# Five pairs of weight blocks multiplied with seven block products in place of eight

## The chip, the core and the metric

The kernel runs on one core of one Trainium2 chip. The metric is the device time of one execution in microseconds (us), the median over several runs. Before the change it is 1874.03 us (three runs, 1873.88 to 1874.24).

## What is computed

The reference is a trunk of two layers over 256 tokens of 2048 channels, in float32. Each layer normalises the input, projects it with one wide matrix, runs a convolution branch and an attention branch, and merges both. Only the end of a layer matters here:

```python
y_conv = conv_branch(...) @ w_proj_conv          # (256, 2048) @ (2048, 2048)
y_mla = mla_branch(...) @ w_proj_mla
y = jax.nn.sigmoid(g_conv) * y_conv + jax.nn.sigmoid(g_mla) * y_mla
return x + y @ w_out                             # (256, 2048) @ (2048, 2048)
```

The two products with `w_proj_conv` (called pconv below) and `w_out` (called wout) are the last two projections of a layer.

## The kernel before

**Work and tiles.** Each projection is a list of blocks of 512 output columns: pconv and wout have four each, and they come last in a layer, in the order pmla 0 to 3, pconv 0 to 3, wout 0 to 3. Behind wout 3 of layer 0 comes the block glu 0 of layer 1. A block is fed by eight pieces of weights. A piece is two K tiles of 128 rows (`KS = 2`) by 512 columns, 512 KB in float32. The 256 tokens are two halves of 128 (`t`).

**Split terms.** Float32 accuracy is had from operands in the fp32r format. Both sides are split into a high and a low part, and of the four products three are computed: high x high, low activation x high weight, high activation x low weight. A piece therefore costs two halves by two K tiles by three terms, twelve matmuls of 512 columns, all accumulated in two PSUM banks, one for each half.

**How a piece gets there.** SP's queue loads it into one of five buffers `raw` (`load`, line 185). ScalarE copies it to `hi`, which rounds it (`split_hi`, line 194, four buffers). VectorE subtracts, `lo = raw - hi` (`split_lo`, line 230, three buffers). `product` (line 362) goes through the pieces: for piece i it issues `hi` up to i+3, `lo` up to i+2 and loads up to i+7, then the matmuls, then `background` (line 266). The order of the twelve matmuls is that of `order_of_products` (line 303): the eight with the high weights first, then the four with the low ones. The last piece of a block ends the first half earlier.

**The order of everything else.** Every engine runs its instructions in the order in which the program issues them (class `InOrder`, line 121). Work beside the matmuls is a list `steps` of functions with the clock at which they are due, one tick of the clock for each piece. `background` runs what is due, in the order of the list. `at_slot(n, f)` (line 247) puts a function n ticks ahead at the end of the list; the evacuation of a block is put at the front (line 394), due one tick after the block's end, or in its last tick for pconv 3 and wout 3.

**Evacuation.** `pconv_evac` (line 1245) multiplies each half in PSUM by a gate and adds another tile (four VectorE instructions of 512 columns, called gates below). The result must be transposed for wout: `turn` (line 418) writes it to DRAM in four transfers, fetches it back 4 ticks later into a tile `turned` of the pool `wide`, has VectorE transpose it 8 ticks later, and one tick later ScalarE and VectorE split it into the high and low parts of `yT`. `turn4` (line 1159) shortens this to 2 and 4 ticks for the last block. `wout_evac` (line 1274) does the same with the layer's output in layer 0, adds the residual `xres`, and makes `hT`, the activations of layer 1, with eight short instructions on ScalarE and eight on VectorE for each block. The last block of layer 1 goes through `last_product` (line 319).

**PSUM.** Four banks are `acc` (two blocks in turn), two are `tp` and one is `s0`, both used by attention only.

Of the kernel before, what the change touches and what calls it, by code (L numbers as in the profile page):

```python
# [11 lines left out]
F32 = mybir.dt.float32  # L12
F32R = mybir.dt.float32r
# [6 lines left out]
P = 128  # L20
T = 2
# [48 lines left out]

REVOLUTION_PIECES = 6


def revolution_pieces():

# [42 lines left out]
def trunk(ctx: ExitStack, tc: tile.TileContext, xT, x, g_in, pos, win, wuq, wukv, wpc, wpm, wo, cst, rows, invf, out):  # L118
# [43 lines left out]
    pieces = []  # L162

    def plan(layer, stream):
        ap, nk = streams[stream]
        i, at = taken.get((layer, stream), (0, 0))
        n = blocks_of_layer()[stream][i]
        mine = []
        for g in range(nk // KS):
            size = P * KS * n  # L170
            pieces.append((ap[layer, at : at + size].rearrange("(p k c) -> p k c", p=P, k=KS), n))
            at += size
            mine.append(len(pieces) - 1)
        taken[layer, stream] = (i + 1, at)
        return nk, n, mine


    plans = []
    for l in range(DEPTH):
        plans.append([(k, i, plan(l, s)) for k, i, s in order_of_layer()])  # L180

    loaded, highs, pairs_of, done, blocks_begun = {}, {}, {}, {}, [0]
    LOAD_AHEAD, HI_AHEAD, LO_AHEAD = 4, 3, 2

    def load(i):
        if i >= len(pieces) or i in loaded:
            return
        ap, n = pieces[i]
        loaded[i] = t = raw_p.tile([P, KS, n], F32, tag="raw", name=f"raw{i}")
        for a in range(0, KS, 1 if i < N_SINGLE else KS):  # L190
            k = slice(a, a + 1 if i < N_SINGLE else KS)
            sp.dma_start(t[:, k, :], ap[:, k, :])

    def split_hi(i):
        if i >= len(pieces) or i in highs:
            return
        load(i)
        n = pieces[i][1]
        paired = n == PAIRED
        both = split_p.tile([P, KS, 2 * n if paired else n], F32R, tag="hi", name=f"hi{i}", bufs=4)  # L200
        highs[i] = both[:, :, :n]
        if paired:
            pairs_of[i] = both
        singly = i < N_SINGLE
        if i == 0:
            one = [slice(a, a + 1) for a in range(KS)]
            scale_x(0, "hi", vec)
            scale_x(0, "lo", vec)
            act.copy(highs[i][:, one[0]], loaded[i][:, one[0]])
            scale_x(1, "hi", vec)  # L210
            act.copy(highs[i][:, one[1]], loaded[i][:, one[1]])
            split_lo(i, one[0])
            scale_x(1, "lo", vec)
            split_lo(i, one[1])
        for a in () if i == 0 else range(0, KS, 1 if singly else KS):
            k = slice(a, a + 1 if singly else KS)

            if singly:
                act.copy(highs[i][:, k], loaded[i][:, k])
            for c in range(min(i * KS + k.start, NCT), min(i * KS + k.stop, NCT)):  # L220
                scale_x(c, "hi", act)
                scale_x(c, "lo", vec)
            if singly:
                split_lo(i, k)
            else:
                act.copy(highs[i][:, k], loaded[i][:, k])
        for a in range(1, LOAD_AHEAD + 1):
            load(i + a)

    def split_lo(i, k=slice(0, KS)):  # L230
        if i >= len(pieces) or done.get(i, (0, 0, 0))[2] >= k.stop:
            return
        n = pieces[i][1]
# [4 lines left out]
        vec.tensor_sub(lo[:, k], loaded[i][:, k], highs[i][:, k].bitcast(F32))  # L238
        done[i] = highs[i], lo, k.stop


# [21 lines left out]
    def mark(name):  # L263
        marks[name] = clock[0]

    def background(n):
        clock[0] += 1
        slot = (8 * (1.5 * n / 2400 + 0.0133) if n == PAIRED else 12 * (n / 2400 + 0.0133)) - 0.04
        for e, split_us in (("vec", KS * n / 960 + 0.06), ("act", KS * n / 1066 + 0.04)):
            budget[e] = min(budget[e], 0.0) + slot - split_us  # L270
# [47 lines left out]

    def last_product(planned, stat, first_out, early_out, half_out):

        nk, n, mine = planned
# [15 lines left out]

        whole = slice(0, n)
        for j, i in enumerate(mine):
            for a in range(HI_AHEAD + 1):  # L340
                split_hi(i + a)
                if a <= LO_AHEAD:
                    split_lo(i + a)
            if j < len(mine) - 2:
                for t, kk, part in order_of_products(i, False, False):
                    k = j * KS + kk
                    sh, sl = stat(k, t)
                    stationary, w = ((sh, done[i][0]), (sl, done[i][0]), (sh, done[i][1]))[part]
                    pe.matmul(pts[t], stationary, w[:, kk, :], start=k == 0 and part == 0, stop=False)
            elif j == len(mine) - 2:  # L350
                products(j, 0, pts[0], whole, False, False)
                products(j + 1, 0, pts[0], whole, False, True)
                first_out(pts[0])
                products(j, 1, pts[1], whole, False, True)
                early_out(pts[1])
            else:
                for a in range(2):
                    products(j, 1, ends[a], slice(256 * a, 256 * a + 256), True, True)
                    half_out(a, ends[a])
            background(n)  # L360

    def product(planned, stat, evacuate, evac_at=EVAC_AT, costs=(0.0, 0.0), before=None, tardy=None):
        nk, n, mine = planned
        blocks_begun[0] += 1
        pts = [acc_p.tile([P, 512], F32, tag=f"acc{blocks_begun[0] % 2}{t}", name=f"acc{mine[0]}_{t}") for t in range(T)]
# [5 lines left out]
        for j, i in enumerate(mine):  # L371
            for a in range(HI_AHEAD + 1):
                split_hi(i + a)
                if a <= LO_AHEAD:
                    split_lo(i + a)
            hi, lo, _ = done[i]
            if before:
                before(j)
            for t, kk, part in [(t, kk, p) for t in range(T) for p in range(2) for kk in range(KS)] if n == PAIRED else ():
# [5 lines left out]
            for t, kk, part in () if n == PAIRED else order_of_products(i, j == len(mine) - 1, j == tardy):  # L385
# [3 lines left out]
                pe.matmul(  # L389
                    pts[t][:, :n], stationary, w[:, kk, :],  # L390
                    start=k == 0 and part == 0, stop=k == nk - 1 and part == 2,
                )
            if j == len(mine) - 1:
                steps.insert(0, (clock[0] + 1 + evac_at, costs, evac))
            background(n)

    def stat_of(hi, lo):
        return lambda k, t: (hi[:, k, t * P : (t + 1) * P], lo[:, k, t * P : (t + 1) * P])
# [200 lines left out]
    for l in range(DEPTH):  # L599
# [566 lines left out]
        def four(evac_src, dst_hi, dst_lo, c, t):  # L1166
# [144 lines left out]
        for kind, i, pl in planned:  # L1311
            if kind == "glu":
                at = EVAC_AT
                if i == 0 and l == 0:
# [171 lines left out]
```

## Time and profile before

The profiled execution has a span of 1872.0 us from its first to its last instruction, on one core at a mean granted TensorE clock of 1.000. Its own time is not listed; the three timed runs have a median of 1874.03 us, 2.03 us more than the span.

| stretch (us) | block | TensorE busy | VectorE busy | ScalarE busy | DMA share |
|---|---|---|---|---|---|
| 762.94 to 784.70 | pconv 0, layer 0 | 21.76 | 13.64 | 9.50 | 0.60 |
| 806.46 to 828.22 | pconv 2, layer 0 | 21.76 | 14.51 | 9.54 | 0.76 |
| 871.74 to 893.50 | wout 1, layer 0 | 21.76 | 11.00 | 9.79 | 0.88 |
| 893.50 to 915.26 | wout 2, layer 0 | 21.76 | 14.28 | 11.89 | 0.86 |
| 1737.92 to 1759.68 | pconv 2, layer 1 | 21.76 | 14.51 | 9.53 | 0.78 |
| 1803.20 to 1824.96 | wout 1, layer 1 | 21.76 | 11.13 | 8.45 | 0.74 |

How to read the profile: PE is TensorE's matmuls, PEld its weight loads, DVE is VectorE, ACT is ScalarE, POOL is GpSimd, and SP is the queue that issues most transfers. A row of the timeline has the start in us, the duration of the merged instructions, the engine, the line, the operation, the output and inputs by the program's names with their shapes, the count, and in brackets how long the engine sat idle before and what ended that. All instructions carry the line of the helper that issues them (L129), so they are told apart by the names of their tiles. Busy times of matmuls are modelled at their ends and overlap a little.

### The profile page before, as it was taken

Reading aid. Unit: us, or ns where it says so; the run is one execution under the profiler, and the core shown is the slowest. Engines: PE = TensorE matmul, PEld = TensorE weight load, DVE = VectorE, ACT = ScalarE, POOL = GpSimd, SP = SyncE. Lnnn points to the kernel's source line nnn. Section 1 sums busy time; section 2 is a strip of 40 time slices with the busy share of each in tenths; the row PEclk is TensorE's granted clock in tenths of the full one; section 3 lists DMA queues with packets and bytes.
Section 4 is the critical chain, followed back from the end, with each engine's and each line's share of the span. In section 5 each row is a group of like instructions: output and inputs, shape, how many; then the busy total and the mean of one; then the engine's idle time right before and its main releaser. Section 6 shows DMA issues by size and latency. Waiting matters only on the chain.

```text
span 1872.0 us, 26855 instructions
## 1 busy us (share of the span) xinstructions
PE 1867.9 (100%) x8449; PEld 1556.5 (83%) x8449; DVE 1592.3 (85%) x2473; ACT 1345.5 (72%) x2421; POOL 493.3 (26%) x942
## 2 busy tenths in 40 slices
PE   9999999999999999999999999999999999999999
PEld 8888888888888888888888888888888888888887
DVE  6899998898999999766669998888899999995664
ACT  7678888888887766544557689788889877563442
POOL 0155555542200000122221455555322000001210
PEclk9999999999999999999999999999999999999999
DMA  8677877887765566678867787777877556566775
GB/s 325 224 264 249 272 253 243 273 270 230 243 202 194 193 218 209 211 237 281 288 226 224 257 268 258 257 247 267 270 224 254 192 192 206 198 222 209 243 250 166
DMA packets 138959, 445.03 MB, mean 238 GB/s; under 512 B 23680, under 2 KB 29056, under 8 KB 138816
## 3 DMA queue, kind: packets, MB, share of 16 engines
q1 hardware_dynamic: 104976, 359.50, 58.1%
q0 software_dynamic: 32832, 82.62, 13.7%
q8 instruction: 66, 1.08, 0.2%
q10 hardware_dynamic: 1008, 1.20, 0.2%
q14 instruction: 77, 0.63, 0.1%
HBM read 399.18 MB, written 44.04 MB: 237 GB/s over the span
## 4 chain that ended last, share of the span: by engine, by line
PE 100%; DVE 0%; issue 0%
PE acc L129 97%; PE o_ps L129 1%; PE s1w L129 1%; PE s L129 1%; PE warm L129 0%; PE acc_end L129 0%; PE var L129 0%; PE mu L129 0%; DVE xres L129 0%
## 5 line engine op out<-in xcount | busy, mean ns | idle before, releaser
L129 ACT CAST hi<-raw 128x1024 fp32r<-128x1024 f32 (+2 forms) x683 | 698.5, 1028 | 405.4 <-PE acc L129 355.4
L129 DVE TENSOR_TENSOR lo<-raw,hi 128x1024 fp32r<-128x1024 f32 (+2 forms) x667 | 803.0, 1205 | 185.7 <-PE acc L129 145.4
L129 PE MATMUL acc<-hi,hT 128*128 128x512 f32 (+1 forms) x1728 | 421.5, 384 | 0.0
L129 PEld LDWEIGHTS acc<-hi,hT 128*128 128x128 f32 x1728 | 319.5, 188 | 63.4
L129 PE MATMUL acc<-hi,h_hi 128*128 128x512 f32 (+1 forms) x864 | 264.3, 387 | 0.0
L129 PE MATMUL acc<-hi,h_lo 128*128 128x512 f32 (+2 forms) x864 | 259.9, 382 | 0.0
L129 ACT ACTIVATE tap<-u_t,cst 128x256 f32<-128x256 f32 x522 | 227.0, 498 | 5.0 <-DVE v_t L129 5.0
L129 PE MATMUL acc<-lo,h_hi 128*128 128x512 f32 (+1 forms) x832 | 224.7, 386 | 0.0
L129 PE MATMUL acc<-lo,hT 128*128 128x512 f32 (+1 forms) x832 | 224.0, 386 | 0.0
L129 DVE SCALAR_TENSOR_TENSOR v_t<-u_t,cst,v_t 128x256 f32<-128x256 f32 x438 | 187.5, 480 | 2.4
L129 PEld LDWEIGHTS acc<-hi,h_lo 128*128 128x128 f32 x864 | 161.4, 188 | 32.9
L129 POOL DMA_DIRECT2D turned<-turn_d x88 | 49.2, 559 | 526.7 <-DVE v_t L129 335.6
L129 DVE TENSOR_TENSOR v_t<-v_t,tap 128x512 f32<-128x512 f32 x261 | 179.5, 688 | 8.8 <-DVE v_t L129 0.5
L129 PEld LDWEIGHTS acc<-hi,h_hi 128*128 128x128 f32 x864 | 160.3, 188 | 30.8
L129 PEld LDWEIGHTS acc<-lo,h_hi 128*128 128x128 f32 x832 | 155.0, 188 | 31.5 <-DVE lo L129 0.4
L129 PEld LDWEIGHTS acc<-lo,hT 128*128 128x128 f32 x832 | 155.2, 188 | 31.2
L129 POOL DMA_DIRECT2D turn_d<-gate x184 | 100.0, 551 | 290.6 <-DVE gate L129 175.6
L129 PE MATMUL acc<-hi,oT 128*128 128x512 f32 x512 | 127.8, 389 | 0.0
L129 PE MATMUL acc<-hi,ycT 128*128 128x512 f32 x512 | 127.7, 389 | 0.0
L129 PE MATMUL acc<-hi,yT 128*128 128x512 f32 x508 | 126.9, 389 | 0.0
L129 PE MATMUL acc<-hi,qkc 128*128 128x512 f32 x448 | 115.4, 389 | 0.0
L129 PEld LDWEIGHTS acc<-hi,ycT 128*128 128x128 f32 x512 | 96.1, 188 | 19.9
(187 smaller groups left out, 2240.2 us busy)
## 6 DMA issues: line engine op xcount, KB each, us to landing
raw<-in_win SPq DMA_DIRECT2D x397, 512.0 KB, 4.3
raw<-in_wpm SPq DMA_DIRECT2D x64, 512.0 KB, 3.4
raw<-in_wpc SPq DMA_DIRECT2D x64, 512.0 KB, 3.5
raw<-in_wo SPq DMA_DIRECT2D x64, 512.0 KB, 4.5
raw<-in_wukv SPq DMA_DIRECT2D x32, 512.0 KB, 4.2
turned<-turn_d POOLq DMA_DIRECT2D x56, 256.0 KB, 4.7
raw<-in_wuq SPq DMA_DIRECT2D x24, 512.0 KB, 4.3
turn_d<-qk POOLq DMA_DIRECT2D x128, 96.0 KB, 3.6
```

The lines of the kernel that those rows point to most:

```text
L129: ins = getattr(self.engine, name)(*a, **k)
```

## The change

Two neighbouring blocks of a projection, over the same four K tiles (pieces 0 and 1 of either block), are a product of 2x2 block matrices: two halves of tokens, two pieces of K, two blocks of columns. Before, it takes eight block products, each of six matmuls (two K tiles, three terms). After, five such pairs take seven, in the manner of Strassen and Winograd: pconv 2 and 3, wout 0 and 1, wout 2 and 3 in layer 0, and pconv 2 and 3, wout 0 and 1 in layer 1. The other twelve K tiles of these blocks are multiplied as before.

- **Units.** The list of pieces becomes a list of units. A unit is a piece as before, or one of the seven, q1 to q7. q1, q2 and q3 are plain pieces; the weights of q7, q6, q5 and q4 are sums of two tiles, made by VectorE (`form`), in `work2` or in place. Each has its own `hi` and `lo` and six matmuls.
- **Ticks.** q1, q7, q6 and q5 stand in the last four ticks of the block ahead of the pair, each before a plain piece; q2, q4 and q3 in the first three ticks of the pair's first block. A block of a pair has six plain ticks. wout 0 has two of wout 1's pieces as well (eight ticks), and wout 1 then four.
- **Activations.** The differences of the activations are made once for each source (`yc` for pconv, `y` for wout), on VectorE and ScalarE, over three or four ticks (`make_forms`).
- **Joining.** q1's bank is copied to a tile by ScalarE. Behind q6 VectorE makes two combinations, one of which ScalarE copies into q7's bank. Behind q5 VectorE writes two banks. Later matmuls add to what lies there.
- **Banks and buffers.** Pairs use in turn `tp`, `s0` and a new bank `extra`, or the four `acc` banks. `raw` has seven buffers, not five, and POOL's memory for descriptors goes down to 8192 bytes (`dynamic_dma_scratch_size`).
- **One turn.** For pconv 2 the fetch comes 3 and the transposes 6 ticks ahead, not 4 and 8.

```diff
+SEVEN = {(l, kind, i) for l in range(DEPTH) for kind, i in (("pconv", 2), ("wout", 0), ("wout", 2))} - {(DEPTH - 1, "wout", 2)}
-    raw_p = pool("raw", 5)
+    raw_p = pool("raw", 7)
+    extra_p = pool("extra", 1, space=PSUM)
...
+            js = [(j, False) for j in range(2 if first or second else 0, len(block.pieces))]
+            if first and k == "wout" and i == 0:
+                js[2:2] = [(j, True) for j, _ in js[:2]]
+            if second and k == "wout" and i == 1:
+                js = js[2:]
...
+                        if q in ("q1", "q2", "q3"):
+                            of.units[q] = plain({"q1": b11, "q2": b21, "q3": b22}[q])
+                        elif q == "q7":
+                            of.units[q] = summed(of.n, (raw(b12), raw(b22)), None, [b12, b22])
+                        elif q == "q6":
+                            of.units[q] = summed(of.n, (unit("q7"), raw(b11)), None, [])
+                        elif q == "q5":
+                            of.units[q] = summed(of.n, (raw(b12), raw(b11)), raw(b12), [])
+                        else:
+                            of.units[q] = summed(of.n, (unit("q6"), raw(b21)), unit("q6"), [])
...
+        vec.tensor_add(dst, *(value(key) for key in u.terms))
...
+    def prepare(i):
+        for a in range(HI_AHEAD + 1):
+            split_hi(i + a)
+            if a <= LO_AHEAD:
+                split_lo(i + a)
+        form(i + HI_AHEAD + 1)
...
+        if q == "q1":
+            def kept():
+                of.rest = wide_p.tile([P, 512], F32, tag="w", name="rest")
+                act.copy(of.rest, of.banks["q1"])
+
+            at_slot(1, kept, 0.0, 0.5)
+        elif q == "q6":
+            def joined():
+                of.both = wide_p.tile([P, 512], F32, tag="w", name="both")
+                vec.tensor_sub(of.rest, of.rest, of.banks["q6"])
+                vec.tensor_add(of.both, of.rest, of.banks["q7"])
+                late.append(lambda: act.copy(of.banks["q7"], of.both))
+
+            at_slot(1, joined, 1.3, 0.5)
+        elif q == "q5":
+            def shared():
+                vec.tensor_sub(of.banks["q6"], of.banks["q5"], of.rest)
+                vec.tensor_sub(of.banks["q5"], of.banks["q5"], of.both)
+
+            at_slot(1, shared, 1.3)
...
+        for at, tick in enumerate(planned.ticks):
+            for q, i, of in tick[:-1]:
+                prepare(i)
+                one_of_seven(q, i, of)
...
+            if c == 2:
+                return turn(evac_src, 512, None, then=use, then_costs=(0.65, 0.65), fetch_at=3, at=6)
...
-    nc = _bacc.Bacc("TRN2", target_bir_lowering=False, num_devices=1)
+    nc = _bacc.Bacc("TRN2", target_bir_lowering=False, num_devices=1, dynamic_dma_scratch_size=8192)
```

The new functions that the steps below speak of, `make_forms` with its parts:

```python
def whole():
    for name, k in (("a", a), ("b", b)):
        st[name] = wide_p.tile([P, KS, SEQ], F32, tag="w", name=f"whole_{name}")
        vec.tensor_add(st[name], hi[:, k, :].bitcast(F32), lo[:, k, :].bitcast(F32))

def differences():
    xa, xb = st["a"], st["b"]
    vec.tensor_sub(xb[:, :, second], xa[:, :, second], xb[:, :, second])
    vec.tensor_sub(xa[:, :, second], xa[:, :, first], xa[:, :, second])
    vec.tensor_sub(xa[:, :, first], xa[:, :, first], xb[:, :, second])
    vec.tensor_sub(xb[:, :, first], xb[:, :, first], xa[:, :, first])
...
at_slot(begin, whole, 1.3)
at_slot(begin + 1, differences, 1.4)
at_slot(begin + 2, separate, 0.0, 1.0)
```

For pconv they begin in the first tick of pconv 1, for wout in the fifth tick of pconv 2; `separate` has two copies on ScalarE and, one tick later, two subtractions on VectorE.

More of the change, by code (lines that the diff above doesn't have):

```diff
@@ L161, in trunk, with pieces_of @@
     taken = {}
-    pieces = []
-    def plan(layer, stream):
+    sources, units = [], []
+    def pieces_of(layer, stream):
         ap, nk = streams[stream]
@@ new lines, in plain, with summed, plan_all @@
+    def plain(source):
+        units.append(SimpleNamespace(n=sources[source][1], source=source, terms=None, needs=[source]))
+        return len(units) - 1
+    def summed(n, terms, into, needs):
+        units.append(SimpleNamespace(n=n, source=None, terms=terms, into=into, needs=needs))
+        return len(units) - 1
+    def plan_all():
+        blocks = [(l, k, i, pieces_of(l, s)) for l in range(DEPTH) for k, i, s in order_of_layer()]
+        seven, home = None, 0
+        for at, (l, k, i, block) in enumerate(blocks):
+            first = (l, k, i) in SEVEN
+            second = at > 0 and blocks[at - 1][:3] in SEVEN
+            block.home = seven.home if first or second else 0
+            home = block.home
+            front = []
+            if first:
+                (b11, b21), (b12, b22) = block.pieces[:2], blocks[at + 1][3].pieces[:2]
+                front = ["q2", "q4", "q3"]
+            js = [(j, False) for j in range(2 if first or second else 0, len(block.pieces))]
[3 more added lines that the diff above has]
+                js = js[2:]
+            following = blocks[at + 1] if at + 1 < len(blocks) else None
+            tail = []
+            if following and following[:3] in SEVEN:
+                tail = ["q1", "q7", "q6", "q5"]
+                upcoming = SimpleNamespace(units={}, home=1 - home, banks={}, forms=None)
+                upcoming.n = following[3].n
+                upcoming.left, upcoming.right = following[3].pieces[:2], blocks[at + 2][3].pieces[:2]
+                following[3].seven = blocks[at + 2][3].seven = upcoming
+            tails = {js[len(js) - len(tail) + a]: q for a, q in enumerate(tail)}
+            block.begins = upcoming if tail else None
+            for j, right in js:
+                tick = []
+                for q, of in ((front.pop(0) if front else None, seven), (tails.get((j, right)), upcoming if tail else None)):
+                    if q:
+                        (b11, b21), (b12, b22) = of.left, of.right
+                        raw, unit = (lambda a: ("raw", a)), (lambda a: ("unit", of.units[a]))
+                        if q in ("q1", "q2", "q3"):
[8 more added lines that the diff above has]
+                            of.units[q] = summed(of.n, (unit("q6"), raw(b21)), unit("q6"), [])
+                        tick.append((q, of.units[q], of))
+                tick.append((right, plain((blocks[at + 1][3] if right else block).pieces[j]), j))
+                block.ticks.append(tick)
+            if tail:
+                seven = upcoming
+        return blocks
@@ L182, in trunk @@
+    plans = [[] for _ in range(DEPTH)]
+    for l, k, i, block in plan_all():
+        plans[l].append((k, i, block))
     loaded, highs, pairs_of, done, blocks_begun = {}, {}, {}, {}, [0]
     LOAD_AHEAD, HI_AHEAD, LO_AHEAD = 4, 3, 2
+    formed = {}
     def load(i):
-        if i >= len(pieces) or i in loaded:
+        if i >= len(units):
             return
[L188 to L192, printed above, removed]
@@ L194, in split_hi, with value @@
-    def split_hi(i):
-        if i >= len(pieces) or i in highs:
+        for source in units[i].needs:
+            if source in loaded:
+                continue
+            ap, n = sources[source]
+            loaded[source] = t = raw_p.tile([P, KS, n], F32, tag="raw", name=f"raw{source}")
+            for a in range(0, KS, 1 if i < N_SINGLE else KS):
+                k = slice(a, a + 1 if i < N_SINGLE else KS)
+                sp.dma_start(t[:, k, :], ap[:, k, :])
+    def value(key):
+        return loaded[key[1]] if key[0] == "raw" else formed[key[1]]
@@ L196, in split_hi, with form, full @@
+    def form(i):
+        if i >= len(units) or units[i].terms is None or i in formed:
             return
         load(i)
-        n = pieces[i][1]
+        u = units[i]
+        if u.into is None:
+            dst = work2.tile([P, KS, u.n], F32, tag="qk", name=f"sum{i}")
+        else:
+            dst = value(u.into)
+        vec.tensor_add(dst, *(value(key) for key in u.terms))
+        formed[i] = dst
+    def full(i):
+        return formed[i] if units[i].terms else loaded[units[i].source]
@@ L199, in split_hi @@
+    def split_hi(i):
+        if i >= len(units) or i in highs:
+            return
+        load(i)
+        form(i)
+        n = units[i].n
         paired = n == PAIRED
@@ L264, in mark, with background @@
         marks[name] = clock[0]
-    def background(n):
+    def background(n, more=()):
         clock[0] += 1
         slot = (8 * (1.5 * n / 2400 + 0.0133) if n == PAIRED else 12 * (n / 2400 + 0.0133)) - 0.04
-        for e, split_us in (("vec", KS * n / 960 + 0.06), ("act", KS * n / 1066 + 0.04)):
-            budget[e] = min(budget[e], 0.0) + slot - split_us
+        slot += len(more) * 6 * (n / 2400 + 0.0133)
+        split = {"vec": KS * n / 960 + 0.06, "act": KS * n / 1066 + 0.04}
+        for e, split_us in split.items():
+            times = 1 + len(more) + (sum(units[i].terms is not None for i in more) if e == "vec" else 0)
+            budget[e] = min(budget[e], 0.0) + slot - times * split_us
         while True:
@@ new lines, in one_of_seven @@
+    def one_of_seven(q, i, of):
+        if not of.banks:
+            begin_seven(of)
+        bank = of.banks[q]
+        if q in ("q1", "q2", "q4"):
+            parts = [of.stat({"q1": 0, "q2": KS, "q4": KS}[q] + kk, int(q == "q4")) for kk in range(KS)]
+        else:
+            parts = [of.forms(q, kk) for kk in range(KS)]
+        hi, lo, _ = done[i]
+        begins = q in ("q1", "q7", "q6", "q5")
+        terms = [(kk, p) for p in range(3) for kk in range(KS)]
+        for m, (kk, part) in enumerate(terms):
+            sh, sl = parts[kk]
+            stationary, w = ((sh, hi), (sl, hi), (sh, lo))[part]
+            pe.matmul(bank, stationary, w[:, kk, :],
+                start=begins and m == 0, stop=m == len(terms) - 1, skip_group_check=not begins,
+            )
+        if q == "q1":
[15 more added lines that the diff above has]
+            at_slot(1, shared, 1.3)
@@ L367, in evac @@
+    def product(planned, stat, evacuate, evac_at=EVAC_AT, costs=(0.0, 0.0), before=None, tardy=None):
+        nk, n = planned.nk, planned.n
+        seven = getattr(planned, "seven", None)
+        if seven:
+            second = planned.pieces[:2] == seven.right
+            pts = [seven.banks[q] for q in (("q6", "q5") if second else ("q1", "q7"))]
+        else:
+            pts = accumulators(f"acc{planned.pieces[0]}")
         def evac():
@@ L369, in evac @@
                 evacuate(t, pts[t][:, : 2 * n] if n == PAIRED else pts[t][:, :n])
[L371 to L375, printed above, removed]
+        for at, tick in enumerate(planned.ticks):
+            for q, i, of in tick[:-1]:
+                prepare(i)
+                one_of_seven(q, i, of)
+            right, i, j = tick[-1]
+            dst = [seven.banks[q] for q in ("q6", "q5")] if right else pts
+            final = at == len(planned.ticks) - 1
+            prepare(i)
             hi, lo, _ = done[i]
```

89 lines of the change are left out of this document (62 added, 27 removed).

## The prediction

> **What bounds the kernel now.** I read the page first (shares, slices, the chain that ended last), then the busy time of each engine in the blocks that the change touches, then VectorE's queue in order of time.
>
> ```profile
> span 1872.0 us, 26855 instructions
> PE 1867.9 (100%) x8449; PEld 1556.5 (83%) x8449; DVE 1592.3 (85%) x2473; ACT 1345.5 (72%) x2421; POOL 493.3 (26%) x942
> PEclk9999999999999999999999999999999999999999
> PE 100%; DVE 0%; issue 0%
> ```
>
> TensorE is busy from end to end, and the chain that ended last is TensorE alone. So only fewer matmuls can shorten this kernel, and whatever stops TensorE costs its full length. The span is 1872.0 us and the median time 1874.03, so 2.0 us lie around the span; I sum on the span and add the difference to the median.
>
> The question is what room VectorE has in the blocks concerned. Each has 21.76 us of TensorE time, eight pieces of weights with twelve matmuls each (columns: stretch, length, then busy time and count of PE, PEld, DVE, ACT, POOL, clock, DMA share, GB/s):
>
> ```profile
> 784.70:806.46 21.76, 21.76 (x97) 18.02 (x96) 12.30 (x12) 8.42 (x9) 5.47 (x10) 1.00 0.72 242
> 828.22:849.98 21.76, 21.76 (x98) 18.02 (x96) 15.20 (x17) 9.53 (x11) 5.48 (x10) 1.00 0.74 243
> 849.98:871.74 21.76, 21.76 (x98) 18.02 (x96) 16.33 (x19) 10.64 (x13) 3.33 (x6) 1.00 0.84 269
> 915.26:937.02 21.76, 21.76 (x98) 18.02 (x96) 14.97 (x21) 11.63 (x20) 6.57 (x12) 1.00 0.89 291
> ```
>
> These are pconv 1, pconv 3, wout 0 and wout 3 of layer 0. TensorE has no idle time in any. VectorE is busy for 12 to 16 us of 21.76, ScalarE for 8 to 12.
>
> **What goes.** The pace of the matmuls:
>
> ```profile
> 828.22 1.98 PE L129 MATMUL acc<-hi,ycT 128*128 128x512 f32 x8
> 830.03 1.07 PE L129 MATMUL acc<-lo,ycT 128*128 128x512 f32 x4
> 830.94 1.98 PE L129 MATMUL acc<-hi,ycT 128*128 128x512 f32 x8
> ```
>
> From 828.22 to 830.94 are twelve matmuls in 2.72 us: 0.2267 us each. A product of two 2x2 block matrices is eight block products of six matmuls (two K tiles by three split terms). Seven instead of eight save 6 matmuls, 1.36 us, in a pair; five pairs save 30 matmuls, **6.80 us**. No row of the profile makes this uncertain. A block product alone takes TensorE 1.36 us, a piece with one block product (a tick) 4.08 us.
>
> **What comes, on VectorE.** Its queue at the start of pconv 3:
>
> ```profile
> 828.48 1.23 DVE L129 TENSOR_TENSOR lo<-raw,hi 128x1024 fp32r<-128x1024 f32 x1 [1.50 <-PE acc L129]
> 829.62 0.68 DVE L129 TENSOR_TENSOR gate<-acc,sc 128x512 f32<-128x512 f32 x1
> 830.34 0.69 DVE L129 TENSOR_TENSOR gate<-gate,ym 128x512 f32<-128x512 f32 x1
> 830.95 0.68 DVE L129 TENSOR_TENSOR gate<-acc,sc 128x512 f32<-128x512 f32 x1
> 831.66 0.69 DVE L129 TENSOR_TENSOR gate<-gate,ym 128x512 f32<-128x512 f32 x1
> 832.27 1.30 DVE L129 STREAM_TRANSPOSE turned<-turned 128x512 f32<-128x512 f32 x2
> 833.49 1.19 DVE L129 TENSOR_TENSOR lo<-raw,hi 128x1024 fp32r<-128x1024 f32 x1
> 834.60 1.28 DVE L129 TENSOR_TENSOR yT<-turned,yT 128x512 fp32r<-128x512 f32 x2
> 835.79 2.36 DVE L129 TENSOR_TENSOR lo<-raw,hi 128x1024 fp32r<-128x1024 f32 x2
> ```
>
> I count an instruction by the distance to the next start when nothing waits: a `lo` of 1024 elements 1.13 (two take 2.36, one 1.23); 512 elements 0.61, or 0.72 where the next needs its result (829.62, 830.34, 830.95); the four gate instructions 2.65; two transposes 1.22; two yT subtractions 1.20. [...] The rows show the overlap, so I take 1.13.
>
> The nearest row to the sums of weights (128x1024, f32 out) is `lo`: 1.13. To the joins, which read and partly write PSUM, it is the gate row with its PSUM input: 0.61 to 0.72. A pair adds 3 `lo`, 4 sums and 4 joins: 3.4 + 4.5 + 2.5 = 10.4 us. For the half-width subtractions and for ScalarE's part:
>
> ```profile
> 748.21 1.43 DVE L129 TENSOR_TENSOR v_t<-turned,v_t 128x256 f32<-128x256 f32 x4
> L129 ACT CAST hi<-raw 128x1024 fp32r<-128x1024 f32 (+2 forms) x683 | 698.5, 1028 | 405.4 <-PE acc L129 355.4
> ```
>
> The differences of the activations are made four times (two sources, two layers): two whole sums and two `lo` at 0.61, four half-width subtractions at 0.34 (1.43 for four) and 0.11 more since each needs the one before, together 4.2 us. All told some 69 us on VectorE. ScalarE gets 3 casts and 2 copies in a pair, at most 5.1 us if each costs a `hi`. That lies in its idle 10 us of a block, so I cost it at nothing, except where ScalarE must wait for a sum that VectorE makes late.
>
> **Where VectorE's room ends: pconv 3, in both layers.** This block carries the last weights of its own pair and the front half of the next, so its 21.76 us hold six pieces and four block products. I follow VectorE from the block's start to the subtraction for q4, the fifth unit of wout 0. The kernel issues a `lo` two units ahead, so eleven `lo` lie in that stretch: 12.4. Four sums (q7, q6, q5, q4): 4.5. The gates of pconv 2 at the block's start and of pconv 3 at its end, which wait for TensorE's last matmul: 5.3. Transposes and yT of pconv 1: 2.4. The last two `lo` of y's differences: 1.2. The four joins: 2.5. Sum 28.4, with 0.26 at the start (828.22 to 828.48) and 0.10 for the last to finish: 28.75. TensorE wants this `lo` after 21.76 + 1.36 (q2) + 2.72 + 0.91 (four high matmuls of q4) = 26.75. It is late by 2.0 us, and by up to one cast (1.05) more where yT's cast stands behind a cast that waits for a sum; I take **2.6 us**, in each layer: 5.2.
>
> Elsewhere the same sum fits. From pconv 1's fifth piece to pconv 2's third tick are seven ticks, 28.6 us; VectorE has 14 `lo`, 4 sums, 4 joins, one block's gates and one's transposes and yT, 27.9 us. It enters some 1.9 late (pconv 1's first four pieces give TensorE 10.9 and VectorE 4 `lo`, the gates, the differences and a sum, 12.5, from 0.26 on), and leaves 1.2 late. A `lo` that starts with its unit ends 3.8 before TensorE wants it (1.36 + 2.72 + 0.91 - 1.23), so that is no wait. The seven ticks of wout 1 and 2 have 5.2 us beside (14.97 less eight `lo` of 1.22), hence 28.0 of 28.6, and nothing before them is late.
>
> **Where a step now comes too late: glu 0 of layer 1.** With six ticks in wout 3, not eight, the steps counted from wout 2 fall two pieces later into the next block. The rows of before, with glu 0 starting at 937.02:
>
> ```profile
> 937.02 1.98 PE L129 MATMUL acc<-hi,hT 128*128 128x512 f32 x8
> ...
> 941.28 2.18 DVE L129 SCALAR_TENSOR_TENSOR hT<-turned,gains,hT 128x128 fp32r<-128x128 f32 x8
> 943.38 1.22 DVE L129 TENSOR_TENSOR lo<-raw,hi 128x1024 fp32r<-128x1024 f32 x1
> 945.43 1.23 DVE L129 TENSOR_TENSOR lo<-raw,hi 128x1024 fp32r<-128x1024 f32 x1 [0.83 <-issue]
> 949.11 0.71 DVE L129 STREAM_TRANSPOSE turned<-turned 128x512 f32<-128x512 f32 x1 [2.45 <-DMA turned<-turn_d]
> 950.49 0.71 DVE L129 STREAM_TRANSPOSE turned<-turned 128x512 f32<-128x512 f32 x1 [0.67 <-DMA turned<-turn_d]
> 951.12 1.18 DVE L129 TENSOR_TENSOR lo<-raw,hi 128x1024 fp32r<-128x1024 f32 x1
> ```
>
> The eight instructions at 941.28 finish hT for K tiles 8 to 11 (wout 2's columns), in piece 1. They move to piece 3, behind the two transposes for wout 3, which were put into the list earlier. Those wait for their DMA until 949.11 and 950.49, so VectorE is free at 951.12, 14.10 us into the block. TensorE wants the low half of K tiles 8 and 9 at 4 x 2.72 + 0.45 = 11.33. The first two of the eight end about 0.6 after 951.12, at 14.7: TensorE waits 3.4, and 0.2 more for the second half of the rows: **3.6 us**, once. How long depends on the fetch. First these two fetches, then the six of pconv 1 to 3:
>
> ```profile
> DMA to landing us min/median/max: 6.6/6.6/6.6
> DMA to landing us min/median/max: 3.9/4.5/5.6
> ```
>
> With 4.5 the wait would be 2.1 shorter, 1.5 us. I take the row of the place itself.
>
> **What I cost at nothing.** The bytes from HBM are the same. The fetch of pconv 2 moves one piece earlier in POOL's queue and its transposes two earlier; POOL is busy 26%. The halved descriptor memory of POOL's queue and the two more raw buffers change no issue that a row shows waiting on TensorE; if POOL's issues stretched, the transposes would be late, as in the last fence. TensorE's new waits for written PSUM (q4 on ScalarE's copy, q3 on the joins) have a tick or more of lead.
>
> **Sum:** 1874.0 - 6.8 + 5.2 + 3.6 = **1876.0 us** (span 1874.0). A measurement of this kernel can tell about 0.2%, 3.75 us, from no change: this is none, 0.1% slower.
>
> **The rivals.**
> 1. *All hidden*: VectorE's added work fits and the fetch lands early: 1874.0 - 6.8 = 1867.2. For it: both lacks are small beside the sums they come from (2.0 of 28.75). Against: the queue is in order and I found no cover. Chance 0.12.
> 2. *One of the two waits is real*: 1872.4 without the one in glu 0, 1870.8 without those in pconv 3. Without those in pconv 3 and with the short fetch it would be 1868.7. Chance 0.16.
> 3. *Raw buffers: a load that waits for a held piece* (slower). The right block's second piece is kept from q7 to q3, ten units. If the load of the piece behind q3 gets that buffer, it starts when q3's `lo` has ended, 1.4 us into q4's time. It lands 3.5 (wpc) to 4.5 us (wo) later and needs a cast of 1.05, so 6.0 to 7.0, while TensorE is there after 1.36 + 2.72 + 1.36 = 5.44. It decides as soon as the buffers are given in turn.
>
> ```profile
> raw<-in_wpc SPq DMA_DIRECT2D x64, 512.0 KB, 3.5
> raw<-in_wo SPq DMA_DIRECT2D x64, 512.0 KB, 4.5
> ```
>
>    With 0.6 to 1.6 in five pairs, 3 to 8 us: 1881.5 in the middle. For it: DMA share is 0.84 to 0.89 in the wout blocks. Against: seven buffers, of which others are free earlier. Chance 0.20.
> 4. *The clock falls after a gap.*
>
> ```profile
> PE warm L129 <- PEq L1475: 0.8, 1, 0.8
> ```
>
>     If TensorE came back from the 3.6 us gap at half rate for as long again, 1.8 us more would be lost: 1877.8. The trace has one wait of TensorE, at the start, and a full clock throughout, so no row here shows it. [...] Chance 0.08.
> 5. *The seven products are not what runs*: 30 matmuls of 512 columns fewer, or not, would be in the count of instructions. No chance of its own.
>
> **How the numbers follow.** My forecast has 0.44, with its own range from 1872.7 (2 x 2.0 and 1.5) to 1878.5 (2 x 3.1 and 5.1, a fetch 1.5 later still). Over 0.2% faster is below 1870.3: rival 1 and the half of rival 2 that has the short fetch, 0.20. Over 0.2% slower is above 1877.8: rival 3, half of rival 4 and 0.05 from the upper edge of the forecast, 0.29. Between: 0.51. The range, 1867.0 to 1882.0, reaches from rival 1 to just past rival 3's middle; what lies above it is the half of rival 3.
>
> **What would show it.** In the changed profile: 8419 matmuls or near it (some records can be missing). PE waits on `lo`, 2 to 3 us each, a few us into wout 0 of both layers, with VectorE busy without a break through pconv 3; and one wait of PE on hT some 11 us into glu 0 of layer 1, with the transposes waiting for their DMA in front of it. No PE wait in pconv 2 and wout 2. If PE waits on `hi` with ScalarE waiting for a raw load, rival 3 is right; if the clock falls below 1.00 behind a gap, rival 4. A busy PE with none of these and a span of 1865 would prove my sums of VectorE too long.

## The result and the profile after

The changed kernel takes **1884.57 us** (median of four runs, 1882.30 to 1885.11), the kernel before 1873.95: a ratio of 1.0054 with a 95% interval of 1.0040 to 1.0068, 10.6 us slower. The forecast was 1876.0 with a range up to 1882.0, so it fell outside. The profiled execution took 1885.0; its span is 11.2 us longer than that of before.

The page of the changed kernel:

```profile
span 1883.2 us, 26921 instructions
PE 1867.8 (99%) x8419; PEld 1553.0 (82%) x8419; DVE 1657.1 (88%) x2560; ACT 1369.0 (73%) x2454; POOL 494.1 (26%) x942
PEclk9999999999999999999999999999999999999999
PE 97%; DVE 1%; issue 1%; DMA 1%; ACT 0%; SPq 0%; DVEq 0%; ACTq 0%; POOL 0%; POOLq 0%
```

The 30 matmuls are gone (8419, not 8449), yet TensorE is as busy as before (1867.8, not 1867.9). Its busy time should be 6.8 less, 1861.1: most of the difference is matmuls that ran slowly. And the chain now runs through VectorE. What TensorE waited for (total us, times, longest):

```profile
PE left L131 <- DVE lo L131: 4.7, 2, 2.4
PE left L131 <- ACT rest L131: 3.3, 2, 1.6
PE acc L131 <- DVE hT L131: 3.1, 1, 3.1
PE warm L131 <- PEq L1680: 0.8, 1, 0.8
```

The first and third rows are the two waits that the prediction had worked out, 2.6 twice and 3.6. The second is new; the fourth was there before. Each slice of the page's clock row averages 47 us, too coarse to show a dip; short stretches show it (behind the busy times of the five engines come the clock, the DMA share and GB/s; g4, below, says why they begin where they do):

```profile
861.41:864.80 3.39, 1.11 (x5) 0.94 (x6) 3.39 (x5) 1.15 (x2) 1.05 (x2) 1.00 0.79 167
864.82:868.21 3.39, 3.39 (x10) 2.62 (x9) 3.39 (x5) 1.88 (x3) 1.13 (x2) 0.50 0.99 344
950.16:953.55 3.39, 1.05 (x5) 0.55 (x3) 0.97 (x2) 2.13 (x6) 0.00 (x0) 1.00 1.04 419
953.57:956.96 3.39, 2.67 (x6) 2.21 (x7) 3.39 (x10) 1.74 (x6) 0.00 (x0) 0.50 0.49 197
956.98:960.37 3.39, 3.39 (x9) 2.65 (x8) 3.39 (x10) 1.04 (x1) 0.00 (x0) 0.50 0.42 157
1800.07:1803.46 3.39, 1.79 (x8) 1.13 (x7) 3.35 (x6) 2.02 (x3) 2.20 (x4) 1.00 0.34 67
1803.48:1806.88 3.40, 2.62 (x11) 2.17 (x12) 3.40 (x5) 1.94 (x3) 1.13 (x2) 1.00 1.00 264
```

The timeline of TensorE around three of the gaps shows what that costs. First q4 in layer 0, then hT, then q4 in layer 1:

```profile
863.69 0.73 PE L131 MATMUL left<-lo,yT 128*128 128x512 f32 x2 [2.35 <-DVE lo L131]
864.25 3.13 PE L131 MATMUL left<-hi,yT 128*128 128x512 f32 x8
867.18 1.57 PE L131 MATMUL left<-lo,yT 128*128 128x512 f32 x4
868.59 1.07 PE L131 MATMUL right<-hi,form_b 128*128 128x512 f32 x4
...
954.29 2.93 PE L131 MATMUL acc<-hi,hT 128*128 128x512 f32 x6 [3.08 <-DVE hT L131]
957.02 1.91 PE L131 MATMUL acc<-lo,hT 128*128 128x512 f32 x4
958.72 2.78 PE L131 MATMUL acc<-hi,hT 128*128 128x512 f32 x8
961.34 1.07 PE L131 MATMUL acc<-lo,hT 128*128 128x512 f32 x4
...
1804.26 0.72 PE L131 MATMUL left<-lo,yT 128*128 128x512 f32 x2 [2.40 <-DVE lo L131]
1804.82 2.01 PE L131 MATMUL left<-hi,yT 128*128 128x512 f32 x8
1806.67 1.07 PE L131 MATMUL left<-lo,yT 128*128 128x512 f32 x4
```

At 0.2267 us each, the twelve matmuls from 864.25 to 868.59 should take 2.72 and take 4.34: 1.62 lost. The eighteen from 954.29 to 961.34 should take 4.08 and take 7.05: 2.97 lost. Behind the third gap, just as long as the first, nothing is lost.

**The ledger of the span:** 1872.0 - 6.8 (matmuls) + 11.1 (waits: 4.7 + 3.3 + 3.1) + 6.7 (TensorE busy longer: 1867.8 - 1861.1) = 1883.0, measured 1883.2. Of the 6.7, the rows above place 4.6 as slow matmuls. Each of the five gaps also costs about 0.1 on restarting (863.69 to 864.25 is 0.56 for two matmuls, not 0.45), and 0.16 since the last matmul in front of it counts whole (0.39 us, where the next otherwise starts 0.2267 after it): 1.2 together. Two halts too short for the list, at 852.4 and 890.1, make some 0.5; some 0.4 remain.

**The new wait.** ScalarE, VectorE and TensorE in pconv 1 of layer 0, in this order:

```profile
796.00 1.04 ACT L131 CAST hi<-raw 128x1024 fp32r<-128x1024 f32 x1
799.65 1.04 ACT L131 CAST hi<-sum 128x1024 fp32r<-128x1024 f32 x1 [2.61 <-PE acc L131]
800.61 0.58 ACT L131 COPY rest<-left 128x512 f32<-128x512 f32 x1
```

```profile
797.19 1.22 DVE L131 TENSOR_TENSOR lo<-sum,hi 128x1024 fp32r<-128x1024 f32 x1
798.33 1.22 DVE L131 TENSOR_TENSOR sum<-sum,raw 128x1024 f32<-128x1024 f32 x1
```

```profile
796.26 0.61 PE L131 MATMUL left<-lo,ycT 128*128 128x512 f32 x2
801.24 0.97 PE L131 MATMUL left<-hi,form_a 128*128 128x512 f32 x3 [1.64 <-ACT rest L131]
```

`left` is one PSUM tile of two banks: q1 goes into one, q7 into the other. q1 is complete at 796.9 (796.26 + 0.61), and ScalarE is idle for 2.61. But the copy `rest` of q1's bank stands in ScalarE's queue behind the cast of q6's weights, and VectorE makes that sum only by 799.55 (798.33 + 1.22). The cast starts 0.10 later, the copy behind it, and q7's first matmul, which writes the same tile, waits for the copy: 1.64 us, and 1.65 in layer 1. (The bracket names PE acc; its matmuls ended within 0.05 us of the sum. In e3, below, they end 0.22 ahead of the cast, which still starts 0.11 behind the sum, so it is the sum.)

### The profile page after: what moved, and what is told of

It reads as the page before. It is cut to its first block, busy times and chain, and to the rows that moved or that the text cites. A ratio compares the mean times of both kernels' runs of the same rounds, so it can differ in the third digit from the quotient of the medians.

```text
span 1883.2 us, 26921 instructions
## 1 busy us (share of the span) xinstructions
PE 1867.8 (99%) x8419; PEld 1553.0 (82%) x8419; DVE 1657.1 (88%) x2560; ACT 1369.0 (73%) x2454; POOL 494.1 (26%) x942
## 4 chain that ended last, share of the span: by engine, by line
PE 97%; DVE 1%; issue 1%; DMA 1%; ACT 0%; SPq 0%; DVEq 0%; ACTq 0%; POOL 0%; POOLq 0%
PE acc L131 84%; PE left L131 5%; PE right L131 5%; PE o_ps L131 1%; PE s1w L131 1%; PE s L131 1%; DVE lo L131 1%; DMA turned<-turn_d 0%; PE warm L131 0%; DVE gate L131 0%; DVE sum L131 0%; DMA turn_d<-xres 0%; DVE right L131 0%; ACT rest L131 0%; PE acc_end L131 0%
## 5 line engine op out<-in xcount | busy, mean ns | idle before, releaser
L131 PEld LDWEIGHTS acc<-hi,oT 128*128 128x128 f32 x512 | 95.8, 188 | 19.7
L131 POOL DMA_DIRECT2D turn_d<-su x128 | 69.9, 552 | 106.7 <-DVE su L131 96.2
L131 PEld LDWEIGHTS acc<-hi,qkc 128*128 128x128 f32 x448 | 83.5, 188 | 17.0
```

What stands on the lines that cost most here:

```text
L131: ins = getattr(self.engine, name)(*a, **k)
```

## The experiments

Theory: three waits of TensorE (hT, q4 on VectorE in pconv 3 and wout 0, q7 on the copy) and the fall of the clock behind them make up the loss. Rivals: the buffers or the fetches; or VectorE's total, so that a wait undone in one place comes back in another. Each ratio below is to the kernel before, measured beside that run.

**e1: hT two pieces earlier.** In `wout_evac`:

```diff
+            if c == 2:
+                return turn(xt, 512, None, then=use, then_costs=(1.15, 1.3), fetch_at=3, at=6)
             turn4(xt, c, t, use, 1.15, 1.3)
```

> The changed kernel, with wout 2's fetch and transposes in layer 0 moved from 4 and 8 ticks to 3 and 6. Theory (each stop of TensorE costs its length and, behind it, matmuls at half clock): the 3.1 us wait on hT in glu 0 of layer 1 goes, and with it the 3.0 us that the matmuls behind it are slower, so 1884.6 - 6.1 = 1878.5. Rival (VectorE as a whole has too much work, and a wait that is removed comes back elsewhere): 1883 to 1885, with a new wait of about 3 us in the same block or the next. Rival (the slow matmuls come from something else than the gap): 1881.5.

Measured: 1879.83 us, 1.0031 of before (1.0019 to 1.0044), 4.7 less than the changed kernel. The wait on hT is gone and the others are as they were (1.64 twice, 2.39 twice). So this wait cost more than its 3.08.

**e2: q4 one plain piece later in wout 0.**

```diff
-                front = ["q2", "q4", "q3"]
+                front = ["q2", None, "q4", "q3"] if (k, i) == ("wout", 0) else ["q2", "q4", "q3"]
```

> The changed kernel, with q4 and q3 of the pair wout 0 and 1 one tick later (a plain piece of 2.72 us of matmuls stands between q2 and q4). Theory: the two waits on lo in front of q4's low matmuls (2.35 in layer 0, 2.40 in layer 1 in the profile) go, and the 1.8 us of slow matmuls that followed in layer 0: 1884.6 - 6.5 = 1878.1. Rival (VectorE's backlog only meets TensorE a unit later): a wait of 2 us on the next lo, 1883 to 1885.

Measured: 1884.13, 1.0055 (1.0039 to 1.0070). q4 no longer waits; the plain piece in its place does, 2.09 and 2.06. The lack belongs to VectorE's queue, not to q4.

**e3: the copy of q1's bank one tick later**, so that q7 no longer stands behind it.

```diff
-            at_slot(1, kept, 0.0, 0.5)
+            at_slot(2, kept, 0.0, 0.5)
```

> The changed kernel, with ScalarE's copy of q1's bank put one tick later, behind q7's matmuls. Theory (q7 waits because it writes a tile of which another half is still to be copied by ScalarE, which stands behind a cast that waits for VectorE's sum): both waits of 1.65 us go, 1884.6 - 3.3 = 1881.3. Rival (q7 would wait for its own operands then): no wait on the copy, but one on hi or lo of about the same length, 1884 to 1885.

Measured: 1880.12, 1.0032 (1.0020 to 1.0044). TensorE's waits:

```profile
PE left L131 <- DVE lo L131: 4.8, 2, 2.4
PE acc L131 <- DVE hT L131: 2.5, 1, 2.5
PE right L131 <- DVE lo L131: 1.1, 2, 0.5
```

The wait on `rest` is gone in both layers, and half a microsecond in each comes back on q5 in pconv 3. The clock fell behind both gaps of 2.4 this time and not behind the one on hT, so the times of single edits don't simply add up.

**e4: all three.**

> The changed kernel with the three edits together: hT earlier, q4 and q3 of wout 0 later, the copy of q1's bank later. Theory: no wait of TensorE is left but the first, the clock stays at 1.00, and what is left is the saving of 30 matmuls: 1884.6 - 6.1 - 6.5 - 3.3 = 1868.7, at best 1867.2. Rival (VectorE's total work): waits come back, 1873 or more.

Measured: 1875.62, 1.0009 (1.0000 to 1.0017): as the rival said, 1873 or more. What stays is q4's lack, moved by one unit, 2.06 and 2.04, and behind both gaps the clock fell, 1.7 lost each time.

**e5: hT earlier, copy later, and the gates of pconv 3 one tick later**, behind the `lo` that q4 needs.

```diff
-                product(..., lambda t, ps, i=i: pconv_evac(i, t, ps), 0 if i == 3 else EVAC_AT, (2.4, 0.0),
+                product(..., lambda t, ps, i=i: pconv_evac(i, t, ps), EVAC_AT, (2.4, 0.0),
```

> The changed kernel with hT earlier and the copy of q1's bank later, and in place of q4 later: the evacuation of pconv 3 (four gate instructions on VectorE that wait for TensorE's last matmul) one tick later, behind q4's lo. Theory (VectorE's queue up to q4's lo is too long by about 2 us; the gates are 2.65 of it): the wait on lo in wout 0 goes in both layers, 1.1 us of waits in pconv 3 stay, so 1867.2 + 1.1 = 1868.3, up to 1870 with slow matmuls behind what stays. Rival (yT's last quarter, made from these gates, is now the late one): a wait of 2 us or more on yT at wout 0's sixth or seventh piece, 1873 to 1877.

Measured: 1873.53, 0.9995 (0.9986 to 1.0004): no difference from before. The time is in the rival's range, but its wait is not there. q4's wait is gone, no wait of TensorE on yT came, but the queue caught q3 (1.71 and 1.76). The clock stayed at 1.00, and the ledger is waits (5.3) and the small costs of each halt (TensorE is busy 1.4 longer than 1861.1): 1872.0 - 6.8 + 5.3 + 1.4 = 1871.9, measured 1872.0.

**e6: as e5, the sums of wout 0 and 1 on GpSimd.**

```diff
-        vec.tensor_add(dst, *(value(key) for key in u.terms))
+        (gps if u.pool else vec).tensor_add(dst, *(value(key) for key in u.terms))
```

> As the kernel with the gates behind, and the four sums of weights for the pair wout 0 and 1 made by GpSimd, not VectorE. Theory (work on VectorE in pconv 3 is what is scarce): 4.5 us less for VectorE there, no wait of TensorE is left in pconv 3, 1867.2 to 1868. Rival (GpSimd's queue is in order and issues the transfers of the transposes: a sum that takes it several us, or waits for a fetch in front of it, comes too late): waits on hi of a sum, 1870 to 1880.

Measured: 1883.97, 1.0052 (1.0039 to 1.0064), slower than either expectation. TensorE now waits 5.05 and 5.04 for q7's `lo`. GpSimd's rows, then VectorE's, of the same stretch:

```profile
843.39 2.37 POOL L131 TENSOR_TENSOR sum<-sum,raw 128x1024 f32<-128x1024 f32 x1
845.71 2.35 POOL L131 TENSOR_TENSOR raw<-raw,raw 128x1024 f32<-128x1024 f32 x1
```

```profile
842.29 6.86 DVE L131 TENSOR_TENSOR lo<-sum,hi 128x1024 fp32r<-128x1024 f32 x1
```

The sum is not only slower there (2.37, where VectorE took 1.22 for one in the changed kernel). VectorE's own `lo`, which takes 1.22 elsewhere, lasts 6.86 (6.85 in layer 1) and ends 1.1 after GpSimd's second sum. Moving the work gave VectorE nothing: it is busy 1668.1 us with eight sums fewer, 1656.9 in e5.

**e7: as e5, q4 and q3 one plain piece later** (the edits of e5 and e2).

> As e5_gates_behind, and in the first block of wout one plain piece goes ahead of q4 and q3, so that both come one plain piece (2.72 us) later. Theory (the backlog is short and belongs to q3's place): e5's waits of 1.71 and 1.76 on q3's low part are shorter than 2.72, so they go; left are the two of 0.5 in pconv 3 and the 0.8 on ScalarE. Span 1872.0 - 6.8 + 1.1 + 0.8 = 1867.1, time about 1869. Rival (as in e2_q4_later, the backlog meets the next low part in the queue, whichever unit it belongs to): a wait of some 1.5 us on the low part of another unit in the same block, in both layers: time 1872 to 1874, as e5.

Measured: 1873.75, 0.9998 (0.9989 to 1.0007). As the rival said: 1.41 on the plain piece, 0.24 on q3, in both layers. As in e2 and e5, shuffling the order in these ticks only chooses who waits.

**e8: three pairs instead of five**, without wout 0 and 1; hT earlier and copy later.

```diff
-SEVEN = {... (("pconv", 2), ("wout", 0), ("wout", 2))} - {(DEPTH - 1, "wout", 2)}
+SEVEN = {... (("pconv", 2), ("wout", 2))} - {(DEPTH - 1, "wout", 2)}
```

> The changed kernel with three pairs in place of five: those of wout 0 and 1 are left out, so that no block carries the last weights of one pair and the first of the next; and with hT earlier and the copy later. Saved are 18 matmuls, 4.08 us. Theory (the waits come from pconv 3 carrying two pairs): no wait on a low part in wout 0, at most the 0.5 in pconv 3, a full clock: 1874.0 - 4.1 + 0 to 1.1 = 1870 to 1871. Rival (one pair is already more than VectorE's room in its own ticks): waits of 1.5 us or more on low parts or on the copy in pconv 2 or 3 of both layers stay, and the time is 1873 or more.

Measured: **1870.09**, 0.9978 (0.9969 to 0.9987): faster than before by 4.0 us. The page:

```profile
span 1867.8 us, 26896 instructions
PE 1863.7 (100%) x8431; PEld 1552.9 (83%) x8431; DVE 1633.0 (87%) x2530; ACT 1360.2 (73%) x2442; POOL 495.3 (27%) x942
```

Eighteen matmuls fewer should save 4.08; TensorE's busy time falls by 4.2 and the span by 4.2. No wait is left but the one of 0.8 at the start. The same stretch from pconv 3 into wout 0 in before, after and e8 (VectorE's busy time is the third of the five):

```profile
828.00:866.00 38.00, 38.00 (x169) 31.49 (x168) 29.03 (x34) 18.44 (x21) 8.81 (x16) 1.00 0.77 245
```

```profile
828.00:866.00 38.00, 35.59 (x154) 28.72 (x153) 36.01 (x45) 19.81 (x23) 8.66 (x16) 0.98 0.61 189
```

```profile
828.00:866.00 38.00, 38.00 (x169) 31.46 (x169) 28.06 (x34) 17.96 (x20) 8.85 (x16) 1.00 0.81 269
```

In the changed kernel this stretch holds six of the seven products of wout 0 and 1 and the gates of pconv 2 and 3: VectorE is busy 36 of 38 us, and TensorE loses 2.4. In e8 none of a pair's products lies in it. A pair by itself, pconv 2 and 3 in e8, from the fifth piece of pconv 1 to the third tick of pconv 2:

```profile
795.00:824.00 29.00, 29.00 (x130) 24.02 (x129) 28.57 (x33) 18.12 (x20) 5.50 (x10) 1.00 0.69 225
```

VectorE is just as full, 28.57 of 29.00, and TensorE loses nothing: one pair fits, with almost no room left.

**g3: the buffers alone.** The kernel before with `raw_p = pool("raw", 7)` and `dynamic_dma_scratch_size=8192`.

> The kernel before with seven raw buffers in place of five and 8192 bytes for POOL's descriptors, and nothing else of the change: its loads may start earlier. Theory (the buffers cost nothing): 1874.0, within 0.05%, no new wait of TensorE. Rival (earlier loads or smaller descriptor memory delay the fetches of POOL's queue): 1 to 4 us more, with PE waiting on hT, yT or hi somewhere.

Measured: 1874.17, 1.0000 (0.9990 to 1.0009). The buffers cost nothing.

**g1: the kernel before with one step late.** wout 2's transposes in layer 0 two ticks later, as the shorter blocks bring about in the changed kernel:

```diff
+            if c == 2:
+                return turn(xt, 512, None, then=use, then_costs=(1.15, 1.3), at=TURNED_AT + 2)
             turn4(xt, c, t, use, 1.15, 1.3)
```

> The kernel before, eight block products, with one edit: the transposes for wout 2 in layer 0 are due 10 ticks ahead, not 8, so that hT's K tiles 8 to 11 are made in the same tick of glu 0 as in the changed kernel. Theory (the order of the steps alone makes the wait, and the gap alone makes the clock fall): a wait on hT of about 3 us in glu 0 of layer 1 and 2 to 3 us of slow matmuls behind it, 1879 to 1880. Rival (the gap costs only itself): 1877. Rival (the wait needs the seven products' backlog on VectorE): 1874.

Measured: 1878.81, 1.0024 (1.0015 to 1.0033). The gap and the slow matmuls come without any of the seven products:

```profile
951.88 2.93 PE L129 MATMUL acc<-hi,hT 128*128 128x512 f32 x6 [3.01 <-DVE hT L129]
954.61 1.30 PE L129 MATMUL acc<-lo,hT 128*128 128x512 f32 x4
955.75 2.00 PE L129 MATMUL acc<-hi,hT 128*128 128x512 f32 x8
```

The span is 5.2 longer: 3.0 of gap, and 2.2 more of TensorE's busy time (1870.1).

**g2 and g4: gaps made on purpose**, in the kernel before, with additional VectorE work behind the fifth piece of a block:

```diff
+            if busy[0] and j == 4:
+                junk = work.tile([P, 512], F32, tag="junk", name="busy")
+                for _ in range(busy[0]):
+                    vec.tensor_add(junk, busy[1][:, :512], busy[1][:, :512])
```

> The kernel before with 13 to 21 additional additions of 512 columns on VectorE (results unused) behind the fifth piece of fourteen blocks of pconv and wout, so that a later lo comes late and TensorE stops for about 0.9, 1.5, 2.1, 2.7, 3.3, 4.5 and 5.7 us, each twice. Theory: behind a short gap the matmuls run at 0.227 us, behind a longer one some of them at half clock, with the limit between 1.6 us (no slow matmuls seen there) and 2.4 us (seen in one layer, not in the other), and never more than some 3.4 us lost behind one gap. Rival (slow matmuls hang on the place, not on the gap): no relation to the length.

> The kernel before with additions of 512 columns on VectorE behind the fifth piece of twelve blocks, in numbers that should make TensorE wait 0.9 us (once), 1.6 us (six times) and 2.3 us (five times). In g2_gap_ladder 13 of 14 gaps of 2.3 to 8.1 us were followed by slow matmuls that cost 1.6 to 2.9 us whatever the gap's length, and one of 2.3 us by none. Theory (whether the clock falls depends on how much of some stretch of a few us the gap fills, so on its length and on where it begins): none behind 0.9 and 1.6, and behind 2.3 some fall and some don't. Rival (a threshold in the length alone): all of 2.3 fall or none. Span 1872.0 + 22 + 0 to 12 us.

Measured: 1977.03 and 1904.95, one run each. In g2 the gaps came out longer than meant, 2.31 to 8.11 us: thirteen additions took 9.40, 0.72 each. Behind 13 of 14 the clock fell. I measure the loss as the time of the first eighteen matmuls less 4.08: it is 1.6 to 2.9 us whatever the length of the gap (1.75 behind 3.03, 2.89 behind 5.20, 1.68 behind 8.11), within the theory's 3.4, which is half of the 6.82 us at a clock of 0.50 behind hT in the changed kernel. The only one without it was one of 2.31. g4 has short ones:

```profile
832.63 0.73 PE L130 MATMUL acc<-lo,ycT 128*128 128x512 f32 x2 [2.30 <-DVE lo L130]
833.20 0.62 PE L130 MATMUL acc<-hi,ycT 128*128 128x512 f32 x2
833.66 0.62 PE L130 MATMUL acc<-lo,ycT 128*128 128x512 f32 x2
834.12 1.98 PE L130 MATMUL acc<-hi,ycT 128*128 128x512 f32 x8
...
902.43 0.73 PE L130 MATMUL acc<-lo,yT 128*128 128x512 f32 x2 [2.30 <-DVE lo L130]
903.00 0.63 PE L130 MATMUL acc<-hi,yT 128*128 128x512 f32 x2
903.47 0.97 PE L130 MATMUL acc<-lo,yT 128*128 128x512 f32 x2
904.24 3.27 PE L130 MATMUL acc<-hi,yT 128*128 128x512 f32 x8
```

Two gaps of 2.30, one free, the other followed by eight matmuls in 3.27 instead of 1.98. Behind 0.86 and six times 1.58 nothing was lost; of five gaps of 2.30 to 2.67 three cost 1.6 more each. So among these gaps of 2.30 to 2.67 length alone doesn't decide. In the second case the clock even falls 1.1 us after TensorE came back (at 903.54; in e1 1.4 after).

The traces show what went with it here. In the changed kernel the granted clock falls to 0.50 at 864.81 and 953.56 and recovers at 868.22 and 960.38: the first stretch is 3.41 us, the second 6.82, twice that, and from 868.22 to 953.56 is 25 times 3.41. Cut at such points, each trace falls into windows of 3.41 us, which lie differently in each (from 864.81 in the changed kernel to a fall at 903.54 in g4 is 11.35 times 3.41). The traces of the changed kernel, e1 to e7, g1, g2 and g4 have 62 gaps of 0.4 us or more behind the first 20 us. At full clock, wherever TensorE idled 1.95 us or more of one window (28 times), the next window ran at a clock of 0.50; wherever it idled 1.83 or less, the next stayed at 1.00.

So the free gap above is cut into 1.53 and 0.77, and the other lies in one window whole. The clock rows of the changed kernel at the top are such windows: TensorE idles 2.28, 2.34 and 1.60 in those behind which the clock falls, falls, and stays (3.39 less its busy time). One window at 0.50 cost 1.62 us behind q4 and 1.7 in e4, about half of its 3.41. A second one followed where TensorE had idled 0.73 us or more of the first, and none where it had idled 0.42 or less. Behind hT it idled 0.73 and there were two: 2.97 lost. The two cases nearest to the limit, each with the window that follows: e3, idle 1.94 (the row is cut just inside the window), then 0.50; g4, idle 1.82, then 1.00:

```profile
1794.00:1797.39 3.39, 1.45 (x7) 0.87 (x5) 3.36 (x6) 1.66 (x2) 2.20 (x4) 1.00 0.42 82
1797.42:1800.80 3.38, 2.98 (x7) 2.40 (x8) 3.38 (x5) 2.26 (x3) 1.14 (x2) 0.50 0.92 289
```

```profile
1777.36:1780.76 3.40, 1.58 (x7) 0.96 (x6) 3.30 (x5) 0.41 (x1) 0.00 (x0) 1.00 0.00 0
1780.78:1784.17 3.39, 2.92 (x13) 2.39 (x14) 3.39 (x4) 1.05 (x1) 0.00 (x0) 1.00 0.56 180
```

## Why the prediction was wrong

- **The saving was right.** 8419 matmuls; e8 shows the price of a pair cleanly, 4.2 us for three.
- **VectorE's prices were nearly right.** It gained 65 us against some 69 worked out.
- **pconv 3 and wout 0: right**, 2.35 and 2.40 against 2.6 each. e2, e5 and e7 show that the lack is the queue's. e8 shows that it goes with the pair of wout 0 and 1, whose first products lie in pconv 3, a block that another pair has left with six pieces; a pair behind a whole block fits.
- **glu 0: right**, 3.08 against 3.6, by the cause that was named (g1: the order of the steps alone makes it; e1: earlier steps remove it).
- **First step that failed: "TensorE's new waits for written PSUM (q4 on ScalarE's copy, q3 on the joins) have a tick or more of lead".** q7 was left out of the list. It waits for the copy of q1's bank, the releaser that its row names (both banks are one tile), and the copy stood behind a cast of a sum that VectorE makes late. The lateness was in the prediction (VectorE "enters some 1.9 late", and ScalarE cost nothing "except where ScalarE must wait for a sum that VectorE makes late"), but was only held against the `lo` that TensorE reads, not against ScalarE's queue. Measured: 3.3 us. e3 removes this wait.
- **Second step that failed: "whatever stops TensorE costs its full length".** It can cost more, as 2.97 us behind one gap of 3.08 show. A fall of the clock was there as rival 4, but for one gap, with 1.8 us and a chance of 0.08. The 1.8 supposed half rate for as long as the gap itself, which no run shows: the clock was at 0.50 for 3.41 us behind a gap of 2.35 and for 6.82 behind one of 3.08, and g2's losses hardly depend on the length of the gap. Measured: 4.6 us of slow matmuls, 2.97 behind the very gap in question and 1.62 behind the one on q4 in layer 0, which the rival left out; restarts and short halts make the rest of the 6.7. g1 shows it with nothing else changed. Which gaps are hit is chance: the four runs of the changed kernel reach from 1882.30 (mean clock 0.999) to 1885.11 (0.997). Without these 4.6 us the profiled execution would have taken about 1880.4 (1885.0 - 4.6), inside the range, but only because rival 3 had stretched it.
- **The sum** was a span of 1874.0. With 3.3 for q7 and 6.7 for TensorE's longer busy time, less 0.45 and 0.5 for the two waits that were shorter than worked out, it is 1883.1; measured 1883.2.
- **Rival 3 (raw buffers held) did not happen**: the changed kernel has no wait of TensorE on a load or a cast, so the upper end of the range, taken from it, had the wrong reason.

The chance in this lies in where a gap falls among the windows of 3.41 us, as the traces show them: in e2 a gap of 2.06 was followed by slow matmuls, while one of 2.09, cut into 1.41 and 0.67, was not.

What the runs did not settle: whether q7 would still wait if q1's bank were a tile of its own, which share between 1.83 and 1.95 us of a window is the limit, and some 0.4 us of the ledger.

## What to carry to other kernels

When another engine feeds TensorE, sum its queue over the ticks in which added work overlaps, and hold any lateness against every engine that reads the late result, with what is queued behind it there, not only against TensorE. Price a gap of TensorE as these runs measured it: one of 2.0 us or more cost its length and, where the clock fell behind it, 1.5 to 3.0 us more (every gap from 2.67 us on but not every shorter one); one of 1.8 us or less cost its length and some 0.3 (in e5, 1.4 on five of them). A saving that overfills the feeding engine is worth more when applied fewer times: three pairs gained 4.0 us (e8) where five, with the same two waits mended and a third moved, came out even (e5).

## What the hardware showed that I had not expected

- The loss behind a gap hardly depends on its length: 1.6 to 2.9 us behind gaps of 2.3 to 8.1 us. Two gaps of 2.39 in the two layers of one execution of e1 differ: behind the first, fourteen matmuls took 4.91 us, behind the second 3.30. The windows of 3.41 us cut the first into 0.41 and 1.97, the second into 1.30 and 1.09.
- In e6 a `lo` of VectorE took 6.86 us (6.85 in layer 1), in place of 1.22, beside two additions of GpSimd of 2.37 and 2.35. All fifteen `lo` of sums took 29.5 us there, 18.2 in e5. What the two engines share is not shown.
